# Differential attention: dedicated PSUM banks for scores, transposed tiles and outputs in place of six handed out in turn

## The chip, the cores and the metric

The kernel runs on one NeuronCore of a Trainium2 chip. A core has engines that each work off their own queue in order: the tensor engine (PE, matmuls; its weight loads are shown apart as PEld), the vector engine (DVE), the scalar engine (ACT), GpSimd (POOL) and the sync engine (SP), which here mostly issues DMA transfers. They hand work to each other through semaphores. Matmul results go to PSUM, a small memory of which this kernel uses eight banks of 128 x 512 float32; everything else is in SBUF.

The metric is the device time of the whole kernel in microseconds: the median of three runs. A profile of one more execution is at hand, with every instruction's start and duration.

## The reference, cut to what matters

Two transformer layers over 512 tokens of width 1024. Each has a half-step FFN, a mixer, cross-attention to 256 memory tokens and a second half-step FFN, each followed by a layer norm. The mixer of layer 0 is differential attention with 8 heads, two score maps per head, and a norm over each head's output:

```python
def diff_attention(x, w_qkv, w_o, lam_q, lam_k, subln_g, cos, sin, lam_init):
    q, k, v = split(x @ w_qkv)                 # q, k: 8 heads x 2 maps x 64, v: 8 heads x 128
    q, k = rope(q), rope(k)
    lam = exp(sum(lam_q[0]*lam_k[0])) - exp(sum(lam_q[1]*lam_k[1])) + lam_init
    for each block i of 128 query tokens:
        s = einsum(q_block, k) * 64**-0.5      # causal mask
        p = softmax(s)
        a = p[map 0] - lam * p[map 1]
        o = a @ v
    o = o * rsqrt(mean(o**2) + 1e-5) * subln_g * (1 - lam_init)
    return o @ w_o
```

The mixer of layer 1 is a pooling mixer; the change touches only layer 0.

## The kernel before, in words

**Matmuls.** Every operand of the large products is split into a high and a low part (`xh`, `xl`; `wh`, `wl`), the high part copied by ACT (L114, for weights also L308), the low part subtracted by DVE (L115, L310). A product is then three matmuls, recorded at L201, L202 and L203. Two PSUM banks (tag `mm`) hold the large products. The other six are the "aux" banks, three tags `px`, `py`, `yz` with two buffers each; in every stage `aux()` hands them out in turn, so that an allocation waits for whoever read the bank six allocations earlier.

**The differential-attention stage** (about 345 to 575 us) weaves two generators. `da_main` projects v, q and k, head by head, with long runs of matmuls, and at the end multiplies the heads' outputs with the output weights (`ps<-wh,oT` and the like). `da_side` walks 32 steps, one for each head and block of 128 queries, and a step does the following, each a few steps behind the one ahead of it:

- scores (`da_scores`): two tiles `sc`, one for each map, matmuls at L983 and L984. DVE applies the mask and takes the maximum (`p, mx<-sc,mask`, L988, one custom instruction and an accumulator read), which is the last read of the bank; ACT exponentiates (L989); DVE forms the difference of the two maps (L992 to L994)
- turning (`da_turn`, two steps later): p is transposed into `pt` by up to four 128 x 128 transposes (L479) and split into `a` (ACT L114, DVE L115)
- output (`da_out`, three steps later): `po<-v,a`, L1014 and L1015; one `po` serves two steps. After the second of them ACT copies a half of it (L1019), DVE adds the other half (L1020), and ACT squares the two blocks with a sum along the row (L1023). Only the sum is used; the squares themselves are written back into `po`
- after a head's four blocks POOL makes the norm's factor `f` (L1030 to L1033), ACT scales `o` (L1039), and `o` is transposed into another `pt` and split into `oT` (ACT L119, DVE L120), of which there are 11 buffers

A step so takes two banks for scores, one for p, half a one for the output and a quarter for the head's transposed output: 3.75 aux banks.

**Around the stage.** At its start the last tokens of the layer norm before are still being turned: `turn` also takes its `pt` from `aux()` (`pt<-ident,X`, split into `xh` and `xl`). At its end `mem`, the memory tokens for cross-attention, is loaded and turned (`pt<-ident,p`, L1234), in aux banks too, followed by the layer norm and the key and value projections `pk`, `pv` of the cross-attention stage.

**The order.** The weave decides from costs in nanoseconds when the side work may follow (constants `GAP` and `LEAD`); a scheduler then fixes each engine's queue at build time, with knowledge of which bank an allocation waits for. On the chip every engine executes its queue strictly as it was fixed, waiting on semaphores.

Of the kernel before, what the change touches and what calls it, by code (L numbers as in the profile page):

```python
# [9 lines left out]
F32 = mybir.dt.float32  # L10
F32R = mybir.dt.float32r
I32 = mybir.dt.int32
AF = mybir.ActivationFunctionType
ALU = mybir.AluOpType
AX = mybir.AxisListType
PSUM = bass.MemoryType.PSUM

P = 128
D = 1024
S = 512  # L20
# [79 lines left out]
def drain(units):  # L100
    for _ in units:
        pass


class Trunk:
# [54 lines left out]
            yield  # L160

    @contextmanager
    def stage_pools(self, w, raw, order):

        with ExitStack() as ctx:
            self.stage = {}
            for n in order:
                if n == order[0]:
                    self.to_w(ctx)
                if n == "mem":  # L170
                    self.to_x(ctx)
                self.stage[n] = ctx.enter_context(self.pool(n))
            self.banks = {n: ctx.enter_context(self.pool(n, space=PSUM)) for n in ("px", "py", "yz")}
            self.w_bufs, self.raw_bufs, self.aux_turn = w, raw, 0
            self.w_order, self.raw_order = [("wh", "wl")], ["raw"]
            self.w_turn = self.raw_turn = 0
            yield
# [4 lines left out]
    def mm(self, name):  # L182
        return self.mmp.tile([P, S], F32, tag="mm", name=name)

    def aux(self, name, tag=None):
        if tag is None:
            tag = list(self.banks)[self.aux_turn % 3]
            self.aux_turn += 1
        return self.banks[tag].tile([P, S], F32, tag=tag, name=name, bufs=2)

    def small(self, tag, shape=(P, 2)):
        return self.smallp.tile(list(shape), F32, tag=tag, name=tag)
# [812 lines left out]
    def da_out(self, st, i):  # L1005
        nc = self.nc
        if i == 0:
            st["o"], st["sq"] = self.tmp("o", (P, NT, P)), self.small("sq", (P, NT))
        if i % 2 == 0:
            st["po"] = self.aux("po").rearrange("p (i s e) -> p i s e", i=2, s=2)  # L1010
        a, o, po, mm = st.pop(("a", i)), st["o"], st["po"], nc.tensor.matmul
        for j in range(i + 1):
            v = st["v"][j][:, st["h"] % 2]
            mm(po[:, i % 2], a[0][:, j], v, start=j == 0, stop=False)  # L1014
            mm(po[:, i % 2, 0], a[1][:, j], v[:, 0], start=False, stop=j == i)  # L1015
        if i % 2 == 0:
            return
        o2 = o[:, i - 1 : i + 1]
        nc.scalar.copy(o2, po[:, :, 1])  # L1019
        nc.vector.tensor_tensor(o2, o2, po[:, :, 0], ALU.add)  # L1020
        sq = st["sq"]
        for i in range(i - 1, i + 1):
            nc.scalar.activation(  # L1023
                po[:, 0, 0], o[:, i], AF.Square, scale=float(P**-0.5), accum_out=sq[:, i : i + 1]
            )
        if i < NT - 1:
            return

        f, G, s0 = self.small("f", (P, NT)), nc.gpsimd, st["sm"][:, :, 0]
        G.tensor_scalar(f, s0, EPS, None, ALU.mult)  # L1030
        G.tensor_tensor(f, f, s0, ALU.mult)
        G.tensor_tensor(f, f, sq, ALU.add)
        G.tensor_tensor(f, f, self.mhalf, ALU.pow)  # L1033
        st["f"] = f
# [34 lines left out]
    def da_side(self):  # L1069

        n = DA_H * NT
        self.mask = self.tmp("mask")
        self.nc.gpsimd.memset(self.mask[:, : S - P], 0.0)
        self.nc.sync.dma_start(self.mask[:, S - P :], self.a["mask"])
        for s in range(n + LS + 2):
            h, i = divmod(s, NT)
            if s < n:
                while h >= len(self.heads) or self.clock < self.heads[h][0] + LEAD:
                    yield WAIT
                self.da_scores(self.heads[h][1], i)  # L1080
                yield W_SC[i]
            h, i = divmod(s - LT, NT)
            if 0 <= s - LT < n:
                self.da_turn(self.heads[h][1], i)
                yield W_T[i]
            h, i = divmod(s - LO, NT)
            if 0 <= s - LO < n:
                while len(self.heads[h][1]["v"]) < NT:
                    yield WAIT
                self.da_out(self.heads[h][1], i)  # L1090
                yield W_O[i]
            h, i = divmod(s - LS, NT)
            if 0 <= s - LS < n and i == NT - 1:
                self.da_scale(self.heads[h][1])
                yield W_E[0]
            h, i = divmod(s - LS - 1, NT)
            if 0 <= s - LS - 1 < n and i == NT - 1:
                self.oT[h] = self.da_turn_out(self.heads[h][1])
                yield W_E[1]
# [342 lines left out]
    def ffn_pools(self):  # L1442
        return self.stage_pools(dict(wh=4, wl=4), dict(ra=4, rc=3), ("wh", "wl", "ra", "rc"))

    def other_pools(self):
        return self.stage_pools(dict(wh=5, wl=5), dict(raw=2), ("wh", "wl", "raw"))

    def late_pools(self):
        order = ("wl", "wh", "raw", "rawe", "mem", "we")
# [20 lines left out]

    def mixer(self, layer, ln):
        if layer == 0:
            bufs = dict(low=4, rt=2, a=4, p=4, o=1, qk=8, _x=0, v=4, oT=11, mask=1)
            with self.other_pools(), self.phase_pool(("v", "v"), "rt", **bufs):
                self.diff_attention(layer, ln)
            self.close_side()
        else:
            w = self.a["xa_wkv"][layer]
            self.later = ExitStack()
            self.later.enter_context(self.late_pools())  # L1480
            self.kvp = self.later.enter_context(self.pool("kv"))
            with self.phase_pool(("pooled", "pooled"), "sq", pooled=20, sq=1):
                with self.tc.high_priority():
                    keys = self.load_cols(w, 0, "rawe")
                    self.load_memory()
                    ahead = [self.halves(t, "we", "we") for t in keys]
                    self.pool_weights()
                    self.raw_order = ["rawe", "raw", "raw"]
                side = self.pool_mixer(layer, ln)
                next(side)  # L1490
                self.kv = []
                self.weave(self.first_heads(layer, ahead), side, 900, 6000)
                drain(self.early_kv(layer, (1,), self.ahead))
            self.close_side()
# [40 lines left out]
```

## Time and profile before

| | |
|---|---|
| median of three runs | 1939.11 us (1938.22 to 1941.71) |
| the profiled execution, its own time | 1943.24 us |
| its span, from the first to the last instruction | 1941.4 us |
| PE busy over the span | 98 % |
| mean granted TensorE clock | 0.997 |
| differential-attention stage | about 345 to 575 us |

The profile gives for each engine its busy time. The chain of waits is followed back from the last instruction, at each step to what released it. In the views by time a row is: start, duration, engine, line, operation, `out<-in`, shape, count, and in brackets the idle time of the engine before it with what ended that idle time. Matmuls overlap in the pipeline, so the duration of one is longer than the distance to the next. In the lists of the queues' order below there are no times: a row is only a line, an operation and its tiles.

### The profile page before, as it was taken

Reading aid. Unit: us, or ns where it says so; the run is one execution under the profiler, and the core shown is the slowest. Engines: PE = TensorE matmul, PEld = TensorE weight load, DVE = VectorE, ACT = ScalarE, POOL = GpSimd, SP = SyncE. Lnnn points to the kernel's source line nnn. Section 1 sums busy time; section 2 is a strip of 40 time slices with the busy share of each in tenths; the row PEclk is TensorE's granted clock in tenths of the full one; section 3 lists DMA queues with packets and bytes.
Section 4 is the critical chain, followed back from the end, with each engine's and each line's share of the span. In section 5 each row is a group of like instructions: output and inputs, shape, how many; then the busy total and the mean of one; then the engine's idle time right before and its main releaser. Section 6 shows DMA issues by size and latency. Waiting matters only on the chain.

```text
span 1941.4 us, 32397 instructions
## 1 busy us (share of the span) xinstructions
PE 1906.5 (98%) x12988; PEld 1740.4 (90%) x12988; DVE 1558.0 (80%) x2262; ACT 1013.7 (52%) x1537; POOL 332.8 (17%) x318
## 2 busy tenths in 40 slices
PE   9899999999999999999999999999999999999998
PEld 8899998888888888989998999999898889999996
DVE  7988987788867557798888888888886568888886
ACT  6554553467755434555554555455454436555552
POOL 2212121111211002312210322112110013111211
PEclk9999999999999999999999999999999999999999
DMA  9878782322136325977695588778444337777861
GB/s 252 195 168 181 167 163 66 91 66 87 44 109 194 110 65 145 223 171 152 145 198 141 106 210 174 174 162 164 143 151 142 109 87 121 187 175 169 185 142 44
DMA packets 254183, 280.59 MB, mean 145 GB/s; under 512 B 9168, under 2 KB 221648, under 8 KB 254032
## 3 DMA queue, kind: packets, MB, share of 16 engines
q0 software_dynamic: 95808, 102.77, 32.5%
q1 hardware_dynamic: 158224, 175.74, 28.5%
q8 instruction: 102, 1.67, 0.4%
q14 instruction: 49, 0.40, 0.1%
HBM read 274.28 MB, written 4.20 MB: 143 GB/s over the span
## 4 chain that ended last, share of the span: by engine, by line
PE 73%; DVE 15%; DMA 5%; ACT 4%; issue 2%; POOL 1%; SPq 0%; DVEq 0%; POOLq 0%; ACTq 0%
PE x L202 6%; PE x L201 6%; PE x L203 6%; PE z L201 4%; PE z L202 4%; PE z L203 4%; PE ps L203 3%; PE ps L202 3%; PE ps L201 3%; DVE wl L115 3%; DMA ra<-in_ffn_w_in_dram 3%; PE px L201 2%; PE px L203 2%; PE px L202 2%; PE xq L202 2%
## 5 line engine op out<-in xcount | busy, mean ns | idle before, releaser
L636 POOL DMA_DIRECT2D ra<-in_ffn_w_in_dram x132 | 170.4, 1314 | 991.6 <-DVE wl L115 829.0
L114 ACT CAST wh<-ra 128x1024 fp32r<-128x1024 f32 x184 | 193.3, 1053 | 211.2 <-PE x L202 59.4
L115 DVE TENSOR_TENSOR wl<-ra,wh 128x1024 fp32r<-128x1024 f32 x184 | 223.5, 1220 | 70.4 <-ACT wh L114 69.6
L114 ACT CAST wh<-rc 128x1024 fp32r<-128x1024 f32 x136 | 142.8, 1053 | 122.2 <-PE x L202 43.5
L201 PE MATMUL x<-xh,wh 128*128 128x256 f32 x704 | 196.1, 279 | 1.7 <-ACT xh L114 0.8
L203 PE MATMUL x<-xh,wl 128*128 128x256 f32 x704 | 195.6, 278 | 1.9 <-DVE wl L115 1.9
L203 PE MATMUL x<-xe,wl 128*128 128x256 f32 x704 | 195.2, 277 | 1.5 <-DVE wl L115 1.5
L202 PE MATMUL x<-xl,wh 128*128 128x256 f32 x704 | 195.6, 278 | 0.3 <-DVE xl L115 0.3
L201 PE MATMUL x<-xe,wh 128*128 128x256 f32 x704 | 195.3, 277 | 0.0
L202 PE MATMUL x<-xe,wh 128*128 128x256 f32 x704 | 195.1, 277 | 0.0
L114 ACT CAST wh<-b 128x1024 fp32r<-128x1024 f32 x112 | 117.8, 1051 | 131.1 <-PE x L202 62.9
L115 DVE TENSOR_TENSOR wl<-rc,wh 128x1024 fp32r<-128x1024 f32 x136 | 164.4, 1218 | 24.6 <-ACT wh L114 24.6
L115 DVE TENSOR_TENSOR wl<-b,wh 128x1024 fp32r<-128x1024 f32 x112 | 136.7, 1220 | 41.4 <-ACT wh L114 41.4
L201 PEld LDWEIGHTS x<-xh,wh 128*128 128x128 f32 x704 | 132.2, 188 | 3.7 <-ACT xh L114 1.1
L203 PEld LDWEIGHTS x<-xh,wl 128*128 128x128 f32 x704 | 132.4, 188 | 2.4 <-DVE wl L115 2.3
L202 PEld LDWEIGHTS x<-xl,wh 128*128 128x128 f32 x704 | 132.6, 188 | 2.1 <-DVE xl L115 0.8
L203 PEld LDWEIGHTS x<-xe,wl 128*128 128x128 f32 x704 | 132.5, 188 | 1.7 <-DVE wl L115 1.7
L202 PEld LDWEIGHTS x<-xe,wh 128*128 128x128 f32 x704 | 132.5, 188 | 1.3
L201 PEld LDWEIGHTS x<-xe,wh 128*128 128x128 f32 x704 | 132.1, 188 | 1.4
L203 PE MATMUL y<-xh,wl 128*128 128x256 f32 x352 | 98.9, 281 | 4.5 <-DVE wl L115 3.7
L201 PE MATMUL y<-xh,wh 128*128 128x256 f32 x352 | 98.1, 279 | 0.1
L201 PE MATMUL z<-xe,wh 128*128 128x256 f32 x352 | 97.8, 278 | 0.4 <-ACT ha L689 0.4
(402 smaller groups left out, 6057.7 us busy)
## 6 DMA issues: line engine op xcount, KB each, us to landing
ra<-in_ffn_w_in_dram POOLq DMA_DIRECT2D x132, 512.0 KB, 6.8
rc<-in_ffn_w_in_dram SPq DMA_DIRECT2D x88, 512.0 KB, 6.0
b<-in_ffn_w_out_dram SPq DMA_DIRECT2D x60, 512.0 KB, 4.9
ra<-in_ffn_w_in_dram SPq DMA_DIRECT2D x44, 512.0 KB, 4.9
rc<-in_ffn_w_in_dram POOLq DMA_DIRECT2D x44, 512.0 KB, 7.0
b<-in_ffn_w_out_dram POOLq DMA_DIRECT2D x16, 512.0 KB, 12.7
raw<-in_da_w_qkv_dram SPq DMA_DIRECT2D x16, 512.0 KB, 5.2
raw<-in_xa_wkv_dram SPq DMA_DIRECT2D x8, 1024.0 KB, 5.8
```

Source lines behind the costliest of these rows:

```text
L114: self.nc.scalar.copy(hi, src),
L115: self.nc.vector.tensor_sub(lo, src, hi.bitcast(F32)),
L201: mm(out, w[0], x[0], start=start, stop=False, skip_group_check=again)
L202: mm(out, w[0], x[1], start=False, stop=False, skip_group_check=again)
L203: self.last_mm = mm(out, w[1], x[0], start=False, stop=stop, skip_group_check=again)
L636: self.last_more = nc.gpsimd.dma_start(t, source(*block), accum_op=ALU.add)
```

## The change

In the differential-attention stage the six aux banks are no longer handed out in turn. `stage_pools` takes a table of homes; the mixer of layer 0 passes `pt=2, sc=3, po=1`, and `aux("sc")` then draws on three banks that hold only scores, `aux("pt")` on two that hold only transposed tiles (those of p, of the heads' outputs, of X at the start and of `mem` at the end), `aux("po")` on one. All other stages keep the three tags with two buffers each. The squares go to a tile of 128 x 128 in SBUF, `sq`, in place of `po`.

```diff
-    def stage_pools(self, w, raw, order):
+    def stage_pools(self, w, raw, order, **homes):
...
-            self.banks = {n: ctx.enter_context(self.pool(n, space=PSUM)) for n in ("px", "py", "yz")}
+            self.homes = homes or dict(px=2, py=2, yz=2)
+            self.banks = {n: ctx.enter_context(self.pool(n, space=PSUM)) for n in self.homes}
...
     def aux(self, name, tag=None):
-        if tag is None:
+        if tag is None and name in self.homes:
+            tag = name
+        elif tag is None:
             tag = list(self.banks)[self.aux_turn % 3]
             self.aux_turn += 1
-        return self.banks[tag].tile([P, S], F32, tag=tag, name=name, bufs=2)
+        return self.banks[tag].tile([P, S], F32, tag=tag, name=name, bufs=self.homes[tag])
...
             nc.scalar.activation(
-                po[:, 0, 0], o[:, i], AF.Square, scale=float(P**-0.5), accum_out=sq[:, i : i + 1]
+                self.squares, o[:, i], AF.Square, scale=float(P**-0.5), accum_out=sq[:, i : i + 1]
             )
...
-        self.mask = self.tmp("mask")
+        self.mask, self.squares = self.tmp("mask"), self.tmp("sq", (P, P))
...
-    def other_pools(self):
-        return self.stage_pools(dict(wh=5, wl=5), dict(raw=2), ("wh", "wl", "raw"))
+    def other_pools(self, **homes):
+        return self.stage_pools(dict(wh=5, wl=5), dict(raw=2), ("wh", "wl", "raw"), **homes)
...
-            bufs = dict(low=4, rt=2, a=4, p=4, o=1, qk=8, _x=0, v=4, oT=11, mask=1)
-            with self.other_pools(), self.phase_pool(("v", "v"), "rt", **bufs):
+            bufs = dict(low=4, rt=2, a=4, p=4, o=1, qk=8, _x=0, v=4, oT=11, mask=1, sq=1)
+            banks = dict(pt=2, sc=3, po=1)
+            with self.other_pools(**banks), self.phase_pool(("v", "v"), "rt", **bufs):
```

Since the scheduler knows which bank a tile waits for, it fixes some of the queues' order otherwise. In the middle of the stage the order stays nearly as it was; it moves at three places. Lines after the edits are three or four higher in the changed kernel (L201 to L203 are L204 to L206 there, L479 is L482, L1014 and L1015 are L1017 and L1018).

The first place is PE's queue at the start of the stage, where the last two groups of tokens, X_78 and X_79, are turned between matmuls of the first v projection. Before:

```order
L479 MATMUL pt<-ident,X_78 128x128 x8
L479 MATMUL pt<-ident,X_79 128x128 x8
L201 MATMUL v<-wh,xh 128x256
L202 MATMUL v<-wl,xh 128x256
L201 MATMUL q<-xh,wh 128x512
L203 MATMUL v<-wh,xl 128x256
```

In the changed kernel:

```order
L482 MATMUL pt<-ident,X_78 128x128 x8
L204 MATMUL v<-wh,xh 128x256
L205 MATMUL v<-wl,xh 128x256
L482 MATMUL pt<-ident,X_79 128x128 x4
L206 MATMUL v<-wh,xl 128x256
L204 MATMUL v<-wh,xh 128x256
L482 MATMUL pt<-ident,X_79 128x128 x4
L205 MATMUL v<-wl,xh 128x256
```

The transposes of X_79 stand behind the first two v matmuls, and their two tiles apart; the q matmul that stood early comes later.

The second place is PE's queue near the end of the stage, where the last block's p is turned while the output projection `ps<-wh,oT` runs. Before:

```order
L479 MATMUL pt<-ident,p 128x128 x4
L201 MATMUL ps<-wh,oT 128x512
L202 MATMUL ps<-wl,oT 128x512
L203 MATMUL ps<-wh,oT 128x512
L1014 MATMUL po<-v,a 128x256
L1015 MATMUL po<-v,a 128x128
L1014 MATMUL po<-v,a 128x256
L1015 MATMUL po<-v,a 128x128
L1014 MATMUL po<-v,a 128x256
L1015 MATMUL po<-v,a 128x128
L201 MATMUL ps<-wh,oT 128x512
```

In the changed kernel:

```order
L204 MATMUL ps<-wh,oT 128x512
L205 MATMUL ps<-wl,oT 128x512
L206 MATMUL ps<-wh,oT 128x512
L1017 MATMUL po<-v,a 128x256
L1018 MATMUL po<-v,a 128x128
L1017 MATMUL po<-v,a 128x256
L1018 MATMUL po<-v,a 128x128
L1017 MATMUL po<-v,a 128x256
L1018 MATMUL po<-v,a 128x128
L482 MATMUL pt<-ident,p 128x128 x4
L204 MATMUL ps<-wh,oT 128x512
```

The four transposes of the last p stand behind three `ps` and six `po` matmuls. A little further down, eight of the sixteen transposes of `mem` (L1237 in the changed kernel) stand among the `ps<-qk,oT` matmuls that follow; before, all sixteen stood in the layer norm.

The third place is DVE's queue in the layer norm behind the stage (X_78 and X_79 are groups of tokens, `wl` the low parts of cross-attention weights, the `mem` tiles the low parts of the memory tokens). Before:

```order
L423 SCALAR_TENSOR_TENSOR X_78<-X_78,mean,v 128x1024
L115 TENSOR_TENSOR mem_6715<-pt,mem_6715 128x512
L425 SCALAR_TENSOR_TENSOR X_78<-X_78,rstd,v 128x1024
L115 TENSOR_TENSOR xl<-pt,xh 128x4x128 x2
L397 SCALAR_TENSOR_TENSOR X_79,sums<-X_79,ps 128x512
L115 TENSOR_TENSOR mem_6699<-pt,mem_6699 128x512
L115 TENSOR_TENSOR mem_6707<-pt,mem_6707 128x512
L115 TENSOR_TENSOR mem_6723<-pt,mem_6723 128x512
L406 TENSOR_SCALAR mean<-sums 128x1
L243 TENSOR_TENSOR wl<-raw,wh 128x1024
```

In the changed kernel:

```order
L426 SCALAR_TENSOR_TENSOR X_78<-X_78,mean,v 128x1024
L115 TENSOR_TENSOR xl<-pt,xh 128x4x128
L428 SCALAR_TENSOR_TENSOR X_78<-X_78,rstd,v 128x1024
L115 TENSOR_TENSOR xl<-pt,xh 128x4x128
L400 SCALAR_TENSOR_TENSOR X_79,sums<-X_79,ps 128x512
L246 TENSOR_TENSOR wl<-raw,wh 128x1024
L115 TENSOR_TENSOR mem_6704<-pt,mem_6704 128x512
L115 TENSOR_TENSOR mem_6728<-pt,mem_6728 128x512
L409 TENSOR_SCALAR mean<-sums 128x1
```

Two of the four `mem` subtractions are gone from here, to some 20 rows earlier; the two `xl` have the second product of X_78 between them, and a `wl` of 1024 columns stands ahead of the first `mem` subtraction that is left.

## The prediction

> **What bounds the kernel now.** The page's chain that ended last comes first, for the whole kernel, and then the same chain inside the stage, because the stage has another limit than the kernel. In the stage's chain a row is start, duration, engine, tile, line.
>
> ```profile
> PE 73%; DVE 15%; DMA 5%; ACT 4%; issue 2%; POOL 1%; SPq 0%; DVEq 0%; POOLq 0%; ACTq 0%
> ...
> 410.75 0.76 DVE rt L941 x2
> ...
> 522.47 0.48 DVE a L115
> 524.91 0.44 PE pt L479 x4
> ```
>
> Over the kernel PE is the bound: 73 % of the chain. In the stage it is otherwise. From 410.75 to 522.95 the chain runs through DVE, ACT and POOL alone, 112 us in which no PE row lies on it; from 524.91 on it is PE's again. PE is busy there nearly all the time, and still not what the end waits for. Two further views say how PE stands to that chain: its waits between 370 and 600 us (us in total, times, longest), and the stretch with the longest of them (busy times by engine, then the granted clock).
>
> ```profile
> PE sc L983 <- DVE a L115: 3.6, 4, 2.5
> ...
> PE sc L983 <- ACT qk L970: 0.2, 1, 0.2
> ...
> 480.00:510.00 30.00, 27.54 (x142) 23.04 (x141) 26.87 (x69) 21.69 (x56) 6.59 (x7) 0.94 0.12 43
> ...
> 500.82 0.55 PE L983 MATMUL sc<-qk 128*128 128x256 f32 x1 [2.46 <-DVE a L115]
> ...
> 520.12 0.19 PEld L1015 LDWEIGHTS po<-v,a 128*128 128x128 f32 x1 [0.18 <-DVE a L115]
> ```
>
> The first line is what three banks for scores are to remove: a score waits for a bank whose last reader is the subtraction of an `a`, 3.6 us in four waits, the longest 2.46 us before 500.82. The others show that PE comes back to the chain all the same: at 520.12 it waits for an `a` as data, which no bank changes. A PE that starts 500.82 earlier meets the chain's times 20 us later and waits there. So removed waits inside 410 to 523 buy next to nothing, while an edit that makes PE late ahead of 410, lengthens ACT's squares on the chain, or makes PE late behind 525, adds its time to the end. That is the sum to make.
>
> **The start of the stage.** With two banks for `pt`, the two tiles of X_79 wait for the reads of X_78's.
>
> ```profile
> 352.66 0.86 PEld L479 LDWEIGHTS pt<-ident,X 128*128 128x128 f32 x8 [0.38 <-DVE X L425]
> ...
> 355.85 2.48 DVE L115 TENSOR_TENSOR xl<-pt,xh 128x512 fp32r<-128x512 f32 x4
> ...
> 356.59 0.39 PE L203 MATMUL v<-wh,xl 128*128 128x256 f32 x1 [0.55 <-DVE xl L115]
> ...
> 363.56 1.29 DVE L310 TENSOR_TENSOR wl<-raw,wh 128x512 fp32r<-128x512 f32 x2 [5.23 <-ACT wh L308]
> ...
> 562.59 0.24 PE ps L201
> ```
>
> Before, the eight transposes (0.9 us, first row) and one q matmul of 512 columns (0.24, the kind of the last row) filled time in which PE waited for `xl` anyway: it resumes at 356.59. Now the transposes wait for the first `xl` (a quarter of 2.48 after 355.85, 356.5) and PE does both after that. No wait follows into which they could go, and DVE, idle for 5.23 us before 363.56, shifts with the q and k it is fed. **+1.1 us.** Bounds: 0, if the wait for `xl` shortens by as much, since only two `xl` are needed for the first matmuls; 1.8, if the transposes run at half clock.
>
> **The first scores.** Three banks for scores are fewer than the six that a score could get before. Where DVE lags, at the first head, this binds.
>
> ```profile
> 383.69 0.28 PE L983 MATMUL sc<-qk 128*128 128x256 f32 x1
> ...
> 385.33 0.33 PE L983 MATMUL sc<-qk 128*128 128x384 f32 x1
> ...
> 386.14 0.29 DVE L988 CUSTOM_DVE_ANT_0 p<-sc,mask 128x128 f32<-128x128 f32 x1
> ...
> 386.35 0.42 DVE L988 CUSTOM_DVE_ANT_0 p<-sc,mask 128x256 f32<-128x256 f32 x1
> ```
>
> The fifth score tile starts at 385.33. Its bank is that of the second, which DVE reads until 386.43 (386.14 + 0.29). The sixth waits equally for the third (386.35 + 0.42). PE is late by **+1.1 us**, in matmuls that run without a gap until 410, where DVE's `rt` waits for a q. Bounds: 0, if DVE's other work there moves behind the reads; 1.5, if the fourth tile's wait on the first adds.
>
> **The squares.** [...] Writing to PSUM and to SBUF differ:
>
> ```profile
> 386.47 0.40 ACT L989 ACTIVATE p<-p,mx 128x128 f32<-128x128 f32 x1 [0.77 <-DVE mx L988]
> 386.78 0.19 ACT L989 ACTIVATION_READ_ACCUMULATOR p<-p,mx 128x1 f32 x1
> ...
> 562.15 0.28 ACT L1023 ACTIVATE po<-o 128x128 f32<-128x128 f32 x1 [0.92 <-DVE o L1020]
> 562.37 0.19 ACT L1023 ACTIVATION_READ_ACCUMULATOR po<-o 128x1 f32 x1
> ...
> 442.15 0.41 ACT po L1023 x2
> ...
> 453.06 0.41 ACT po L1023 x2
> ...
> 462.81 0.41 ACT po L1023 x2
> ...
> 514.74 0.28 ACT po L1023
> ```
>
> An exponential of the same shape into SBUF takes 0.40 with its read at +0.31; a square into PSUM 0.28 with its read at +0.22. A square so costs 0.09 more (bounds 0, if only the operation differs, and 0.12). On the stage's chain stand the pairs at 442.15, 453.06 and 462.81, the square at 514.74, and one like it near 479: eight. **+0.7 us** (bounds 0 and 1.0). The other 24 lie beside other work, on an ACT that is idle for 8.3 of 30 us in the stretch quoted; without that cover they would be 2.2 us more.
>
> **One bank for outputs.** It comes free with DVE's addition, no longer with the second square.
>
> ```profile
> 525.83 0.42 DVE L1020 TENSOR_TENSOR o<-o,po 128x256 f32<-128x256 f32 x1
> ...
> 526.21 0.28 PE L1014 MATMUL po<-v,a 128*128 128x256 f32 x1
> ```
>
> At one place the next `po` comes first, at 526.21, while the addition ends at 526.25: with the semaphore **+0.1 us** (bounds 0 and 0.5; PE is the chain there).
>
> **The end of the stage.** Two `pt` banks meet the last turns, one of them held by a head's transposed output until an `oT` buffer is free.
>
> ```profile
> 558.00 0.49 PE L479 MATMUL pt<-ident,p 128*128 128x128 f32 x3
> ...
> 558.38 0.42 DVE L115 TENSOR_TENSOR a<-pt,a 128x256 fp32r<-128x256 f32 x1
> ...
> 561.99 0.60 PE L479 MATMUL pt<-ident,p 128*128 128x128 f32 x4
> ...
> 563.40 0.74 DVE L120 SCALAR_TENSOR_TENSOR oT<-pt,subg,oT 128x512 fp32r<-128x512 f32 x1
> ...
> 564.06 0.68 DVE L115 TENSOR_TENSOR a<-pt,a 128x512 fp32r<-128x512 f32 x1
> ...
> 565.84 0.37 ACT L1019 COPY o<-po 128x256 f32<-128x256 f32 x1 [1.79 <-PE po L1015]
> ...
> 569.48 0.33 PE L479 MATMUL pt<-ident,o 128*128 128x128 f32 x1 [1.09 <-ACT o L1039]
> ...
> 574.61 0.39 PE L201 MATMUL ps<-low,oT 128*128 128x512 f32 x1
> ```
>
> The `pt` of 558.00 now waits for the `a` that ends at 558.80, and PE is 1.0 late with the next. The last p (561.99 before) stands behind three `ps` and six `po` and waits for the `oT` of 563.40; in the new order it runs at about 564.5. Behind it DVE makes an `oT` (0.74) before the `a`, which ends at 567.1 instead of 564.74. So the copy of 565.84 comes 2.6 later, with the pair of squares (0.2) the transpose of 569.48 comes 2.8 later, at 572.3. PE has more to do ahead of it than before and hides part of this. After it there remain 12 matmuls of 0.24, three transposes and eight of `mem` at about 0.1: 4.1 us, to 576.4, where the trace has the next stretch begin at 574.61. **+1.8 us.** Bounds: 0.3, if `a` and `oT` change places in effect; 2.8, if nothing hides it.
>
> **The layer norm behind it.** Half the `mem` transposes are gone from here, yet they had filled waits.
>
> ```profile
> 594.43 1.27 DVE L115 TENSOR_TENSOR xl<-pt,xh 128x512 fp32r<-128x512 f32 x2
> ...
> 596.23 0.68 DVE L115 TENSOR_TENSOR mem<-pt,mem 128x512 fp32r<-128x512 f32 x1
> ...
> 596.96 0.39 PE L202 MATMUL pk<-mem,wh 128*128 128x256 f32 x1
> ...
> 598.39 1.22 DVE L243 TENSOR_TENSOR wl<-raw,wh 128x1024 fp32r<-128x1024 f32 x1
> ```
>
> The `pk` of 596.96 waits for the low part of `mem` (596.23 + 0.68). DVE's new order puts the `wl` (1.22) ahead of it and has one `mem` (0.6) less in front: 0.6 later on DVE. **+0.5 us**, bounds −1.9 (PE's idle time between 589 and 597 us gone, since eight transposes less are waited for) and 1.0. Behind 606 us the order is that of before and PE has no gap that would take the delay back.
>
> The sum: 1.1 + 1.1 + 0.7 + 0.1 + 1.8 + 0.5 = 5.3 us. The profiled execution took 1943.24, 4.1 above the median, 1939.11; so 1948.5 against it and **1944.4 us** for the median.
>
> **The rivals.**
>
> *PE gets ahead (faster).* If DVE and ACT find their inputs earlier when PE no longer stops, the 3.6 us of waits are won, and with the gap before 500.82 the half clock behind it: 0.06 of 30 us in that row, 1.7. If the early waits do not arise either, 5.3 us less: 1933.8. For it speaks that scores then run ahead whenever DVE works on `a`; against it that no PE row lies on 112 us of chain, and the wait at 520.12 for data. It decides if DVE's idle times in the stage turn out to end on PE. Chance 0.13.
>
> *Only the early terms count.* The end and the layer norm are the terms that rest on a moved order, and the one's loss may be the other's gain (bounds 0.3 and −1.9). Then 1.1 + 1.1 + 0.7 + 0.1 = 3.0: 1942.1. Chance 0.27.
>
> *A half clock in the layer norm.* In the new order PE has some 1.1 us of work in 4.8, from the last `ps` (594.6, with the delay) to the late `mem` (599.4). The trace had such a gap once, 2.46 us, and the clock was half behind it. A second such stretch adds 1.7: 7.0 in all, 1946.1. Chance 0.20. The Trainium skill ("TensorE: Matmul & The Clock Gate", What's actually happening) lets the clock fall only after a whole idle window of about 3.4 us, at windows that run freely; by that rule a stretch with transposes in it costs nothing. The gap before 500.82, shorter than such a window, was followed by the half clock all the same, so the trace does not agree, and the rule lowers no chance here.
>
> *The change does not do what it says.* Banks never bind beyond what they did, the squares hide, PE meets the chain where it did: within 1 us of before, about 1939.5. The waits at 383 to 386 and at 558 speak against it. Chance 0.07.
>
> **How the numbers follow.** The forecast has 0.33. Two results of this kernel can be told apart by about 0.2 %, 3.9 us: faster is below 1935.2, slower above 1943.0. Slower: 0.33 + 0.20 = 0.53. Same: 0.27 + 0.07 = 0.34. Faster: 0.13. The forecast's own range is 1943 to 1946.5, from the bounds of the end and the layer norm taken half. The range that holds 8 in 10 goes from 1937 (the rival in which the early terms count, with part of the layer norm's idle time won) to 1949 (the half clock, with the upper bounds of the start and the end); the faster case lies outside.
>
> **What would show it.** Right: PE idle at the fifth score tile, near 387, for about 1 us, ended by a DVE `p`; no wait of scores on `a`; PE waiting for `po` or `qk` instead; DVE's order from 410 to 523 taking the same 112 us and some 0.7 more; waits for DVE before the last turns; a wait of `pk` for `mem`. The forecast is wrong if that stretch becomes shorter by over a microsecond, or if the distance from the last q's `rt` to the first `pk` does not grow.

## The result, and the profile after

The changed kernel takes 1946.54 us (median of seven runs, 1945.3 to 1949.87), the kernel before on the same chips 1941.11 (seven runs, 1938.22 to 1942.3). The ratio is 1.0031, with a 95 % interval of 1.0021 to 1.0040: slower by 5.4 us by the medians and 6.0 by the ratio, and by more than 0.2 %. Forecast were 1944.4 us against 1939.11, a ratio of 1.0027, and a range of 1937 to 1949.

The profiled execution of the changed kernel has a span of 1944.8 us, 3.4 more than the profiled one of before, which was itself one of the longer runs. The first line is the chain that ended last, over the whole kernel; the others are PE's waits between 370 and 600 us.

```profile
PE 75%; DVE 15%; ACT 4%; DMA 3%; issue 2%; POOL 1%; SPq 0%; DVEq 0%; POOLq 0%; ACTq 0%
```

```profile
PE pt L1237 <- DVE xl L115: 1.4, 2, 1.1
PE pk L205 <- DVE mem L115: 1.4, 1, 1.4
PE po L1017 <- ACT a L114: 1.3, 1, 1.3
PE pt L482 <- ACT o L1042: 1.1, 1, 1.1
PE po L1018 <- DVE a L115: 0.9, 2, 0.5
PE po L1017 <- DVE o L1023: 0.8, 2, 0.4
PE sc L986 <- DVE mx L991: 0.7, 2, 0.5
PE pt L482 <- DVE a L115: 0.7, 1, 0.7
```

The waits of a score on an `a` (3.6 us before) are gone, as three score banks promise. In their place PE waits for `po` and its operands, for score banks at the first head, for `pt` at the end, and in the layer norm for `xl` and `mem`.

To see what each costs, take an instruction that both traces have, and subtract its start before from its start now. This lag is the time that the program has lost up to there; what a stage adds is the lag at its end less that at its start. The places below are times in the trace of before, on PE, except where DVE is named; from 390 us (PE) on the table follows DVE's chain, and from 506 us (DVE) on PE again.

| stretch | predicted | the change | what it holds |
|---|---|---|---|
| 349 to 369 | +1.1 | +0.95 | start of the stage |
| 369 to 390 | +1.1 | +1.11 | first scores |
| 390 (PE) to 489 (DVE) | +0.7 in all | +0.01 | DVE's chain with the squares |
| 489 to 506 (DVE) | | −1.09 | one instruction of POOL, see below |
| 506 (DVE) to 530 (PE) | +0.1 | +0.19 | one `po` bank |
| 530 to 574.6 | +1.8 | +1.87 | end of the stage |
| 574.6 to 609 | +0.5 | +2.64 | layer norm, with a half clock |
| sum | +5.3 | +5.68 | |

Ahead of the stage the changed trace is 0.91 us earlier and behind 609 us it gains another 1.4; both lie where neither the code nor the order differs.

The start, PE and then the first scores, in the changed kernel:

```profile
353.64 0.38 PE L204 MATMUL v<-wh,xh 128*128 128x256 f32 x1 [2.02 <-ACT xh L114]
...
355.69 0.87 PE L482 MATMUL pt<-ident,X 128*128 128x128 f32 x4 [1.55 <-DVE xl L115]
...
384.17 0.39 PE L986 MATMUL sc<-qk 128*128 128x256 f32 x1 [0.27 <-DVE mx L991]
386.54 0.44 PE L986 MATMUL sc<-qk 128*128 128x384 f32 x1 [0.46 <-DVE mx L991]
```

The transposes of X_79 wait 1.55 us for `xl`, as said, and the fourth and fifth score tile wait for DVE's read of the first and second. The end of the stage, PE and DVE:

```profile
559.11 0.55 PE L482 MATMUL pt<-ident,p 128*128 128x128 f32 x3 [0.69 <-DVE a L115]
...
564.78 0.66 PE L482 MATMUL pt<-ident,p 128*128 128x128 f32 x4
...
566.75 0.68 DVE L115 TENSOR_TENSOR a<-pt,a 128x512 fp32r<-128x512 f32 x1
...
572.30 0.33 PE L482 MATMUL pt<-ident,o 128*128 128x128 f32 x1 [1.09 <-ACT o L1042]
```

The last p is turned at 564.78 (worked out: 564.5), its `a` ends at 567.4 (567.1), the output's transpose comes at 572.30 (572.3). The layer norm behind, where the large difference lies, in PE's rows and by stretches (busy times by engine, then the granted clock):

```profile
597.27 0.66 PE L1237 MATMUL pt<-ident,p 128*128 128x128 f32 x4 [1.14 <-DVE xl L115]
...
599.62 0.58 PE L205 MATMUL pk<-mem,wh 128*128 128x256 f32 x1 [1.35 <-DVE mem L115]
```

```profile
596.00:599.00 3.00, 1.12 (x8) 0.76 (x6) 3.00 (x6) 2.09 (x4) 0.00 (x0) 0.89 0.55 175
599.00:602.00 3.00, 2.38 (x11) 2.38 (x12) 3.00 (x5) 1.24 (x2) 0.29 (x1) 0.50 0.52 137
602.00:605.00 3.00, 3.00 (x16) 3.00 (x16) 2.56 (x3) 0.00 (x0) 2.06 (x2) 0.50 0.99 342
605.00:608.00 3.00, 3.00 (x28) 3.00 (x28) 2.26 (x3) 2.15 (x3) 0.00 (x0) 0.97 1.07 378
```

PE is busy for 1.12 of 3 us, and then the clock is half for some 6.8 us (0.89, 0.50, 0.50 and 0.97 of four stretches of 3 us). That is the rival "a half clock in the layer norm". It had a chance of 0.20, a price of 1.7 and a time of 1946.1.

A correction to the section on the change: the tiles of `mem` are not drawn from the two `pt` banks. They are turned on the banks of the stage behind, which are handed out in turn over the same memory; the new banks move them only through when that memory comes free.

### The profile page after: what moved, and what is told of

Same layout as the page of the kernel before. It is cut to its first block, busy times and chain, and to the rows that moved or that the text cites. A ratio compares the mean times of both kernels' runs of the same rounds, so it can differ in the third digit from the quotient of the medians.

```text
span 1944.8 us, 32383 instructions
## 1 busy us (share of the span) xinstructions
PE 1910.9 (98%) x12988; PEld 1746.4 (90%) x12988; DVE 1559.3 (80%) x2262; ACT 1014.3 (52%) x1537; POOL 334.0 (17%) x318
## 3 DMA queue, kind: packets, MB, share of 16 engines
q8 instruction: 102, 1.67, 0.4%
## 4 chain that ended last, share of the span: by engine, by line
PE 75%; DVE 15%; ACT 4%; DMA 3%; issue 2%; POOL 1%; SPq 0%; DVEq 0%; POOLq 0%; ACTq 0%
PE x L205 6%; PE x L204 6%; PE x L206 6%; PE z L205 4%; PE z L204 4%; PE z L206 4%; PE ps L206 4%; PE ps L205 4%; PE ps L204 4%; DVE wl L115 3%; PE px L204 2%; PE px L206 2%; PE px L205 2%; PE y L206 2%; PE xq L205 2%
## 5 line engine op out<-in xcount | busy, mean ns | idle before, releaser
L204 PE MATMUL x<-xh,wh 128*128 128x256 f32 x704 | 197.0, 280 | 1.4 <-ACT xh L114 1.4
L206 PE MATMUL x<-xh,wl 128*128 128x256 f32 x704 | 196.6, 279 | 1.1 <-DVE wl L115 1.1
L204 PE MATMUL x<-xe,wh 128*128 128x256 f32 x704 | 195.7, 278 | 0.0
L206 PE MATMUL x<-xe,wl 128*128 128x256 f32 x704 | 195.5, 278 | 0.0
L204 PEld LDWEIGHTS x<-xh,wh 128*128 128x128 f32 x704 | 133.0, 189 | 3.0 <-ACT xh L114 1.7
L206 PEld LDWEIGHTS x<-xh,wl 128*128 128x128 f32 x704 | 133.6, 190 | 1.3 <-DVE wl L115 1.3
L204 PEld LDWEIGHTS x<-xe,wh 128*128 128x128 f32 x704 | 132.6, 188 | 1.4
L206 PEld LDWEIGHTS x<-xe,wl 128*128 128x128 f32 x704 | 132.7, 188 | 0.0
L206 PE MATMUL y<-xh,wl 128*128 128x256 f32 x352 | 99.1, 281 | 2.6 <-DVE wl L115 1.9
L204 PE MATMUL y<-xh,wh 128*128 128x256 f32 x352 | 98.3, 279 | 0.4 <-ACT wh L114 0.4
```

Source lines behind the costliest of these rows:

```text
L204: mm(out, w[0], x[0], start=start, stop=False, skip_group_check=again)
L206: self.last_mm = mm(out, w[1], x[0], start=False, stop=stop, skip_group_check=again)
```

## The experiments

In each, the lags are against the same trace of before. Four ran together with 30 runs of the kernel before, four with 27, two with 21 and one with 14.

**The bank table alone.**

```diff
-                self.squares, o[:, i], AF.Square, ...
+                po[:, 0, 0], o[:, i], AF.Square, ...
```

> The bank table alone; the squares go to PSUM (po) again. Theory from the trace of the change: a pair of squares lasts 0.84 us in PSUM and in SBUF alike, so moving them costs nothing and its use is to free the one po bank earlier. Put back, four po allocations (near 434, 503, 515 and 526 us) wait for the second square 0.1 to 1.6 us longer, 3.1 in sum; the first three lie where PE meets the DVE chain again, so only the last counts: 0.8 us more than the change, about 1947.3 against 1946.5. Rival A (the step of the prediction that squares in SBUF cost 0.7): 0.7 less than the change. Rival B (every wait of PE counts): 3.1 us more, 1949.6.

Measured: 1946.63 us, ratio to before 1.0034 (1.0019 to 1.0050). That is the change's own ratio within the intervals, which do not tell 0.8 us from nothing; 3.1 more and 0.7 less are less likely by the medians and no more. The trace says where the squares' place matters, in PE's waits between 370 and 600 us:

```profile
PE po L1017 <- ACT po L1026: 2.7, 2, 2.1
```

`po` waits for ACT's square, 2.7 us in two waits where the change waits 0.8 us for the addition. Yet DVE's lag from 390 to 506 us grows by no more than in the change: PE waits there beside the chain. From 506 to 530 us this trace loses +1.05 where the change loses +0.19. But its clock is half there, too (0.83 from 516 to 526 us), and two traces below with squares in SBUF and a half clock at that place lose +1.14. So with one `po` bank the SBUF squares do free the bank earlier; whether any of it reaches the end is not shown.

**The squares alone.**

```diff
-            with self.other_pools(**banks), self.phase_pool(...)
+            with self.other_pools(), self.phase_pool(...)
```

> Squares to SBUF alone, six banks in turn as before; the queues' order on every engine is that of before. Theory: no difference to before within 0.2 us on the chain (pairs of squares 0.84 us in both). Rival A (the prediction's step): 0.7 us slower than before, seen as a growing lag of DVE between 442 and 515 us. Rival B: banks come free earlier and the scores' waits on an a shrink from 3.6 us, without a gain in time.

Measured: 1940.38 us, ratio 1.0004 (0.9990 to 1.0017): no difference. A square in SBUF and its reads, here and (two rows behind) in the kernel before:

```profile
439.83 0.31 ACT L1026 ACTIVATE sq<-o 128x128 f32<-128x128 f32 x1 [0.71 <-DVE o L1023]
440.05 0.19 ACT L1026 ACTIVATION_READ_ACCUMULATOR sq<-o 128x1 f32 x1
440.27 0.31 ACT L1026 ACTIVATE sq<-o 128x128 f32<-128x128 f32 x1
```

```profile
442.15 0.28 ACT L1023 ACTIVATE po<-o 128x128 f32<-128x128 f32 x1 [0.71 <-DVE o L1020]
442.37 0.18 ACT L1023 ACTIVATION_READ_ACCUMULATOR po<-o 128x1 f32 x1
442.58 0.28 ACT L1023 ACTIVATE po<-o 128x128 f32<-128x128 f32 x1
```

The square itself is 0.03 longer, but the read starts 0.22 behind it in both, and the second square 0.43 to 0.44. DVE's lag from 390 to 489 us is −0.08. The prediction's step, read from an exponential, falls. The waits of scores on an `a` shrink from 3.6 to 2.5 us here, and nothing is won by it, as the second rival said.

This run has the queues' order of before, so it also shows what differs from one execution to the next. It gains 1.7 us at the start and 1.1 us between 489 and 506 against the profiled execution of before. At the start the clock is the cause: the same stretch from 352 to 361 us, first before and then here:

```profile
352.00:361.00 9.00, 7.02 (x40) 6.03 (x39) 6.33 (x13) 3.95 (x8) 0.00 (x0) 0.81 0.38 122
```

```profile
352.00:361.00 9.00, 7.05 (x54) 6.30 (x55) 5.79 (x13) 4.13 (x7) 0.00 (x0) 1.00 0.37 118
```

Between 489 and 506 it is one power function of POOL on the chain, for a head's norm, before and in the changed kernel:

```profile
492.35 2.12 POOL L1033 TENSOR_TENSOR f<-f,mhalf 128x4 f32<-128x4 f32 x1
```

```profile
493.50 1.04 POOL L1036 TENSOR_TENSOR f<-f,mhalf 128x4 f32<-128x4 f32 x1
```

It took 2.1 us in the trace of before; of the other twelve traces six have the gain of 1.1 us there and six do not. It goes with neither the banks nor the order: the squares alone, in the order of before, have 1.04, and the start undone, with the new banks, has 2.12. So it is not the change; what decides it is not shown.

**The start undone.**

```diff
-        pt = self.aux("pt", "px" if "ra" in self.stage else None)
+        pt = self.aux("pt", "px" if "ra" in self.stage else self.x_home())
...
+    def x_home(self):        # at the start of this stage only
+        self.x_turns = getattr(self, "x_turns", 0) + 1
+        return ("pt", "sc")[self.x_turns % 2]
```

> The change, with the turned tiles of X at the start of the stage drawn from pt and sc banks alternately; PE's order there is that of before, all else that of the change. Theory: the start's loss of 0.95 us (lag of PE at 369 us against 349 us) is gone, the rest stays: 0.95 less than the change, about 1945.6. Rival: the lost time reappears at the first scores because DVE is then further behind (no gain, 1946.5).

Measured: 1944.35 us, ratio 1.0022 (1.0007 to 1.0038). The lag from 349 to 369 us is −1.75 in place of +0.95, with the clock at 1.00 from 352 to 361 us; from 369 to 390 it is +1.11 as in the change. So the loss does not reappear at the first scores. The gain of 2.7 us is more than the 0.95 expected: 1.7 of it is the half clock that this execution does not have. In the layer norm it has the change's half clock (+2.95 from 574.6 to 609).

**The first scores undone.**

```diff
-        sc = [self.aux("sc")[:, :n] for m in range(2)]
+        sc = [self.aux("sc", self.sc_home(st, i, m))[:, :n] for m in range(2)]
...
+    def sc_home(self, st, i, m):     # first head only
+        return {(1, 1): "po", (2, 0): "pt"}.get((i, m))
```

> The change, with the fourth and fifth score tile of the first head drawn from the then unused po and pt banks; all queues' orders are those of the change. Theory: the two waits of sc on DVE near 387 us (1.1 us of lag) are gone and stay gone through the DVE chain from 410 us on: 1.1 less than the change, about 1945.4. Rival: DVE's chain is paced by its own work by then, PE arrives earlier and waits; no gain.

Measured: 1945.53 us, ratio 1.0028 (1.0015 to 1.0041). The lag from 369 to 390 us is +0.02 instead of +1.11, and DVE has the same lag up to 489 us: the 1.1 us pass through the chain in full, the rival falls. But in this execution a new loss of 0.95 us more than in the change arises from 506 to 530. The stretch from 516 to 526 us, first in the change, then here:

```profile
516.00:526.00 10.00, 8.61 (x70) 8.03 (x68) 8.25 (x21) 7.67 (x22) 3.21 (x5) 1.00 0.12 46
```

```profile
516.00:526.00 10.00, 8.59 (x58) 8.19 (x57) 8.28 (x25) 8.47 (x24) 2.28 (x2) 0.83 0.01 2
```

PE is up to 4.2 us earlier than in the trace of before by 506 us (3.0 in the change), which is 3.1 us further ahead of DVE's chain in both, and gives it back in a bunch of waits. In this execution the clock then falls to half (0.83 over the ten microseconds), just where PE becomes the chain again; in the change's it did not.

**The end on other banks.**

```diff
-        pt, o = self.aux("pt"), st.pop("o")
+        tag = "sc" if st["h"] >= 6 else None
+        pt, o = self.aux("pt", tag), st.pop("o")
```

> The change, with the transposed outputs of the last two heads drawn from the sc banks, so that the two pt banks at the end of the stage are for the turned p alone. PE's order there goes back to that of before but for eight transposes of mem that stay in. Theory: the end's 1.9 us (lag of PE at 574.6 us against 549 us) shrinks to the 0.9 us of those transposes; the late mem in the layer norm and the half clock behind it stay: about 1.0 less than the change, 1945.5. Rival: the end waits for ACT's o and not for banks, so that the lag at 574.6 us stays at 1.9.

Measured: 1947.16 us, ratio 1.0031 (1.0018 to 1.0045). The rival's number holds: the lag from 530 to 574.6 us is +2.08. Its reason does not, since the wait for ACT's `o` is as long before (1.1 us) and so adds nothing. The lag arises at two places. +0.92 comes where a `pt` for p waits 0.69 us for DVE's `a`, the wait of the row at 559.11 above: two banks for p alone are still too few there. The rest comes with the eight transposes of `mem`, the only rows of PE's order at the end that are not there before. The half clock of the layer norm is there, too (+1.83 from 574.6 to 609).

**Start, end and layer norm undone.** As the start undone, but `x_home` also in the layer norm behind the stage, together with the edit of the end.

> The bank table kept, but the turned tiles of X (at the start and in the layer norm behind) alternate between pt and sc, and the last two heads' outputs are turned on sc. Four rows of PE's order differ from before. Theory: start, end, late mem and the half clock behind it are gone; left are the first scores (1.1) and the one po bank (0.2): 1.3 slower than before, about 1941.5 where before has 1940.2. Rival: the half clock and the lag come from the few banks themselves, wherever the tiles lie: more than 3 slower than before.

Measured: 1941.55 us, ratio 1.0010 (0.9999 to 1.0021): the time is as expected. Lags: +0.16 at the start (with a half clock, as before), +1.10 at the first scores, +0.19 for `po`, +0.90 at the end and −0.11 in the layer norm. The end was expected to lose nothing. PE's order there is that of before in every row, and all sixteen transposes of `mem` stand in the layer norm again, where no half clock comes; what is left at the end is the wait of a `pt` for DVE's `a` (0.7 us).

**All undone.** The kernel above with the edit of the first scores.

> As the kernel with start and end undone, and the fourth and fifth score tile of the first head on the unused po and pt banks: the table of banks without any of the terms of the sum. Theory: the 3.6 us of waits that three score banks remove lie beside DVE's chain, so the time is that of before within 0.1 percent, 1940.2. Rival: with its costs gone the table shows its gain: 3 us or more faster than before, below 1937.2.

Measured: 1940.34 us, ratio 1.0002 (0.9992 to 1.0011): the time of before within the interval, on the table of dedicated banks. Its waits of PE between 370 and 600 us begin so:

```profile
PE po L1028 <- ACT a L114: 1.3, 1, 1.3
PE pt L493 <- ACT o L1053: 1.1, 1, 1.1
PE pt L1248 <- DVE xl L115: 0.9, 1, 0.9
PE po L1029 <- DVE a L115: 0.9, 2, 0.5
PE po L1028 <- DVE o L1034: 0.8, 2, 0.4
PE pt L493 <- DVE a L115: 0.7, 1, 0.7
```

No score waits for an `a` any more, and nothing is won by it: the interval leaves out the rival's 3 us. DVE's lag from 390 to 489 us is −0.02. The longest wait is now for an `a` as data. Not quite all is undone: the last line is the wait for a `pt` bank at the end, where this trace still loses +0.97, and the one `po` bank costs +0.20. These 1.2 us lie within the interval.

**Matmuls without use in the layer norm.**

```diff
         drain(self.to_tokens(self.oT[4:], self.a["da_w_o"][0], ...))
+        fill, w = self.aux("po"), self.oT[7][0]
+        for n in range(8):
+            self.nc.tensor.matmul(fill, w[:, :P], w, start=True, stop=True)
```

> The change, with eight matmuls of 128 x 512 without use into the po bank, seven of them in PE's order between the last ps of the layer norm and the last transposes of mem, where PE has little to do; four transposes of mem move back into the norm. Theory: PE is late for nothing by it, the half clock from about 598 us (1.4 to 2.9 us of lag in three of four runs of the changed order) does not come: the lag from 588 to 609 us is about 0 to 0.5 in place of 2.6 and more; 2 less than the change, about 1944.5. Rival: the fillers delay the late mem and the time stays or grows by up to 1.6.

Measured: 1945.87 us, ratio 1.0025 (1.0015 to 1.0034). The stretch from 594 to 606 us, the change and then here:

```profile
594.00:606.00 12.00, 9.27 (x49) 8.26 (x48) 11.03 (x14) 6.22 (x9) 3.58 (x3) 0.72 0.60 195
```

```profile
594.00:606.00 12.00, 10.87 (x83) 10.01 (x81) 11.56 (x15) 6.56 (x11) 3.73 (x3) 1.00 0.49 146
```

Seven of the matmuls without use lie in this stretch, with four more transposes of `mem` than in the change, and the clock stays at 1.00. The lag from 574.6 to 609 us is +0.48 in place of +2.64, the prediction's +0.5. PE's wait for `mem` is still there (1.1 us). So the half clock is worth some 2.1 us in the change's profiled execution, and it is likely PE's idle time that brings it; one trace alone does not show that, and the ratios (1.0025 and 1.0031) do not tell the two kernels apart.

**Matmuls without use at the start.**

```diff
         self.turned = self.split(hi[:, :, o], lo[:, :, o], pt)
+        if (t, half) in ((2, 1), (3, 1)):    # start of this stage; po: one tile
+            x = self.xh[0][:, :, :P]
+            for n in range(4):
+                self.nc.tensor.matmul(self.fill, x[:, 0], x, start=True, stop=True)
```

> The change, with eight matmuls of 128 x 512 without use into the po bank, in PE's order between the transposes of X_78 and the first v matmul of the stage's start, where PE waits 2.0 us for xh. Five of five profiles of the changed order at the start have a half clock there for 3.4 to 6.8 us and a lag from 349 to 369 us of 0.95 to 2.1 against the trace of before (which had one, too), while three profiles in the order of before have none and a lag of -1.2 to -1.8. Theory: the fillers fit in the wait, the half clock does not come, and what is left is the work that comes later: a lag from 349 to 369 us of about -0.7 (1.0 above the -1.75 without a half clock); 1.5 to 2.5 less than the change, about 1944.5. Rival: the start's cost is the waits for xh and xl alone, so that the lag stays at 1 to 2 or grows.

Measured: 1945.41 us, ratio 1.0021 (1.0012 to 1.0030). The expectation failed: the lag from 349 to 369 us is +1.13 and the half clock is there.

```profile
351.32 2.10 PE L476 MATMUL po<-xh 128*128 128x512 f32 x8
353.47 0.38 PE L205 MATMUL v<-wh,xh 128*128 128x256 f32 x1
353.69 0.28 PE L206 MATMUL v<-wl,xh 128*128 128x256 f32 x1
355.64 0.94 PE L489 MATMUL pt<-ident,X 128*128 128x128 f32 x4 [1.67 <-DVE xl L116]
356.24 0.56 PE L207 MATMUL v<-wh,xl 128*128 128x256 f32 x1
```

All eight went into the wait for `xh`. The wait for `xl` of 1.67 us stayed open, and a stretch with that alone was enough for the half clock (0.56 for a matmul that takes 0.28 to 0.38 otherwise).

**Matmuls without use in three gaps.** The eight at the start, seven that read the `xh` of X_78 and so come behind the two v matmuls, and the eight of the layer norm.

> The change with matmuls without use in three gaps: eight after the transposes of X_78 and seven behind the first two v matmuls (they read the xh of X_78, and fill the wait of 1.67 us for xl that the eight alone left open; the half clock came all the same), and the eight of the layer norm. The transposes of X_79 stand together here. Theory: no half clock at the start and none in the norm; the lag from 349 to 369 us is -0.7 to -0.3, that from 588 to 609 us 0 to 0.5, the rest as in the change (scores 1.1, end 1.9): about 3.5 less than the change, 1943.5 where before has 1940.5 (ratio 1.0013 to 1.0018). Rival: the clock at the start falls for another reason than PE's idle time, lag 1 to 2 again.

Measured: 1944.88 us, ratio 1.0027 (1.0015 to 1.0039). Both stretches do what the theory says: −0.26 from 349 to 369 us, with the clock at 1.00 from 352 to 361 us, and +0.51 from 574.6 to 609.

```profile
352.00:361.00 9.00, 8.81 (x62) 7.66 (x61) 5.09 (x11) 3.11 (x7) 0.00 (x0) 1.00 0.37 118
```

The time of all does not follow so far: this trace has the half clock of 520 us (+1.14 from 506 to 530), and the interval neither shows nor excludes the 3.5 us.

**All undone, with matmuls without use.** In the kernel with all undone, four such matmuls stand behind the transposes of X_78 and four behind those of X_79.

> The kernel with all terms undone, and four matmuls without use after the transposes of X_78 and four after those of X_79, to keep the clock up at the start. Theory: the half clock of the start, which two of five profiles in that order have (1.7 us each), does not come: 0.7 below the mean of before, 1939.4 where before has 1940.0, hardly measurable. Rival: the first four delay the transposes of X_79 and with them xh by up to 0.9 us: no gain or a loss of as much.

Measured: 1943.39 us, ratio 1.0007 (0.9997 to 1.0017). No half clock at the start (−1.53), but one in the layer norm, of 1.5 us, and no gain that could be measured. No version tried is faster than before.

**The half clock over all traces.** The lag of the start is the one that varies most:

| order at the start | traces | half clock there | lag 349 to 369, us |
|---|---|---|---|
| of before, without useless matmuls | before, squares alone, start undone, start and end undone, all undone | 2 of 5 | 0, −1.73, −1.75, +0.16, −1.23 |
| of the change, gap for `xl` open | the change, banks alone, first scores, end on other banks, both single fillings | 6 of 6 | +0.95, +2.06, +2.04, +1.80, +1.55, +1.13 |
| of the change, both gaps filled | three gaps | 0 of 1 | −0.26 |
| of before, with useless matmuls | all undone with them | 0 of 1 | −1.53 |

In the layer norm six traces have the changed kernel's order with the gap open, and five of them show the half clock, all but that of the banks alone; the two with the gap filled do not. Of the other five, one does (all undone, with matmuls without use). Near 520 us three traces show it, all with the new banks.

Between 320 and 620 us the thirteen traces have eighteen half clocks, thirteen of 3.41 us and five of 6.83. In the 3.41 us ahead of each, PE was busy for 0.79 to 2.04 us. How little is too little is not sharp: near 520 us the stretch ahead had 2.00 us of work in the first-scores trace, and in the trace of the change one of 2.09 (516.41 to 519.82 us) was not followed by a half clock.

## Why the prediction was right, and where it was not

*PE is not the bound between 410 and 523 us, so removed waits there buy next to nothing.* Right, and shown: without the waits DVE's lag from 390 to 489 us is −0.02, and with all but 1.2 us of the table's costs undone the time is that of before, 1.0002 (0.9992 to 1.0011). One of the signs of being wrong came up all the same: in the change's trace the chain from 410.75 to 522.47 us is 1.07 us shorter, and not 0.7 longer. The whole of it is the one instruction of POOL, which is as short in the squares alone.

*The start, +1.1.* The wait and the work that comes after it are as described. The change has +0.95, but against an execution of before that had a half clock at that place. Against the executions without one (−1.23 to −1.75) it is 2.2 to 2.7; with both gaps filled, and so no half clock on either side, 1.0 to 1.5 is left of it, with fifteen matmuls without use in it. The bound of 1.8 for transposes at half clock was the right thought; what was missed is that the changed order brings the half clock in each of six traces and that of before in two of five.

*The first scores, +1.1.* Right: +1.11, undone by two other banks (+0.02), and carried through to 489 us in full. The waits fall on the fourth tile (0.27), which the sum had only in its upper bound, and on the fifth (0.46); the sixth does not wait.

*The squares, +0.7.* Wrong. The step "an exponential of the same shape into SBUF ... with its read at +0.31; a square into PSUM 0.28 with its read at +0.22" took for the destination what belongs to the operation. Measured 0.0. The lower bound had said so ("0, if only the operation differs").

*One bank for outputs, +0.1.* Right: +0.19.

*The end, +1.8.* Right: +1.87, and in its times. The first step, a `pt` that waits for an `a` and makes PE 1.0 late, measured +0.88 to +0.93 in each of the eleven traces with the new table, also with other banks for the last two outputs; so the outputs' hold on a `pt` bank is not needed for it. The other 0.95 goes with the eight transposes of `mem`, which the sum had in its 4.1 us: with PE's order of before and these eight in it the end lost 2.08, without them 0.90. The late turn of the last p adds nothing that these runs show; PE has other work ahead of the transpose of `o`, as the section said.

*The layer norm, +0.5.* Right within its bounds without the half clock (+0.48 with PE's gap filled, +0.10 in the one trace of that order that has no half clock and no filling), and short by 2.1 with it. The likeliest case left it out, and the rival that held it had 0.20, though the same section counted 1.1 us of work in 4.8. That "the trace had such a gap once" overlooks a place: the trace of before has a half clock behind the gap of 2.46 us and another at the start of the stage (0.81 from 352 to 361 us), where PE had been busy for 1.66 of 3.41 us. With both seen, the larger chance was this rival's. Its price, 1.7, was one half clock of 3.4 us; the change's trace has one twice as long.

So the sum came out near (5.3 against 5.68) because two errors of opposite sign stood beside each other: 0.7 for squares that cost nothing and 2.1 for a half clock left to a rival; the instruction of POOL, −1.1, which goes with neither the banks nor the order, made the trace's sum smaller. That the number fits so well is luck: the measured difference of 5.4 to 6.0 us lies between the forecast's 5.3 and the third rival's 7.0, and the composition is that of the third rival. The rule of the Trainium skill that was weighed there ("TensorE: Matmul & The Clock Gate", What's actually happening: half rate after a whole idle window of about 3.4 us) would have priced the layer norm at nothing. The traces do not agree with it: 1.12 us of work in 3, and a single gap of 1.67 us, were followed by the half clock.

*PE gets ahead.* It does get ahead of DVE's chain, by 3.1 us more than before at 506 us in the change and in the first-scores run, and gives it back by 530. DVE's chain is not sooner for it (−0.02 from 390 to 489 us with the costs undone), so its idle times do not end on PE, and the rival falls by its own condition.

## What to carry to other kernels

A wait removed on an engine that is not the chain turns up at the next place where that engine meets the chain; look for that place before counting the gain. Banks that are dedicated to a purpose cost most where the mix is not the steady one, at a stage's start and end, and a planner that knows the banks will move work there; price those ends from the order. And where PE's work becomes thin ahead of a stretch that PE bounds (here 2.0 us or less in 3.4), add the half clock to the price, 1.7 us for each 3.4 us of it: it can be as much as all the waits.

## What the runs showed of the hardware

The half clock needs no window without work: PE was busy for 1.12 us in 3 ahead of it in the layer norm, and at the start one gap of 1.67 us between matmuls was enough; with matmuls without use in the gaps the clock stayed at 1.00 (two traces of two in the layer norm, one of one at the start). Whether it falls in a given execution varies with the same order of instructions (two of five traces, at the start in the order of before), which makes 1.7 us and more of the difference between two profiles with that order. The same power function of POOL took 1.04 us in six traces and 2.12 in seven at the same place. A square of 128 x 128 on ACT takes 0.31 us into SBUF and 0.28 into PSUM, and its row sum can be read equally early, 0.22 behind its start.
